# Moving conditioning passes into the opening of a decoder layer, and loading x by features there

## The chip, the cores and the metric

The kernel runs on one core of one Trainium2 chip. The metric is the time of one execution on the device, in microseconds (us); lower is better. Beside the median of three runs there is one execution under the profiler, and all durations below are from that one.

## What is computed

One decoder layer over 256 tokens of 2048 features. What matters here is its beginning:

```
mod = (silu(c) @ w_ada + b_ada).reshape(9, 2048)       # conditioning: 9 vectors
h = rms_norm(x, norm_ffn1) * (1 + mod[1]) + mod[0]
x = x + 0.5 * mod[2] * swiglu(h, w_ffn1_gu, w_ffn1_down)
h = rms_norm(x, norm_mix) * (1 + mod[4]) + mod[3]
x = x + mod[5] * token_mixing(h, ...)
h = rms_norm(x, norm_ffn2) * (1 + mod[7]) + mod[6]
x = x + 0.5 * mod[8] * swiglu(h, w_ffn2_gu, w_ffn2_down)
return rms_norm(x, norm_final)
```

swiglu(h) is (silu(h @ w_gate) * (h @ w_up)) @ w_down, with 5632 columns for each of gate and up. All is float32.

## The kernel before

**Products.** Every large product is made of three products in the fast float32 format (fp32r): high part by high part, low part of the activations by high part of the weights, and high part of the activations by low part of the weights (`products`, L353; the matmul is L359). Weights come by DMA from SyncE's queue into a ring of four 1 MB buffers (`raws`, tile `raw`); ScalarE casts 1024 columns to the high part (`wh`, L374), VectorE subtracts it to get the low part (`wl`, L376), into a ring of three pairs (`wsp`). One such pair, a piece, feeds 12 matmuls of 512 columns.

**Conditioning.** `w_ada` lies transposed in memory, one row block of 128 outputs by 2048 inputs (1 MB) for each of the 9 vectors and 16 feature blocks. VectorE multiplies such a row by silu(c) and sums it, in passes (`ada_pass`, L216, the instruction is L219): four passes of 512 columns for the vectors made behind other work. `conditioning` (L265) is a generator of 192 passes for the vectors 2, 4 and 3; `tick` (L317), called after each piece, takes as many steps of it as `pace["rate"]` says, and `pace["ahead"]` says how many passes ahead of its use a row is loaded. Where a row goes is said by the function handed in (`place_early`, L1179).

**The opening.** The first FFN can't start on all features at once, since mod[0] and mod[1] need 32 MB of `w_ada`. So it goes through four groups of feature blocks, 0 and 1, 2 to 5, 6 to 11, 12 to 15 (L1120). In each group the loop of L1182 visits 16 chunks of 512 columns of gate and up (`visit`, L1132), adds this group's part of the product to a partial sum (copied to and from SBUF, L1143 and L1170), and between visits the generator `group` (L1037) makes the next group's h: for each pair of feature blocks it loads four rows (`place`, L979) and sums them, scales x by the roots of the mean squares (ScalarE, L1028), turns it on TensorE into two PSUM banks (`turned_x`, L1024, four transposes, L1032), and applies scale and shift on ScalarE (`modulated`, L625). In the third group the 192-pass generator ticks as well: 48 ticks at 2/3, 32 passes, each row into `ring[1]`, one single buffer, loaded when its first pass is due. The remaining 160 passes stand behind the 117 ticks that follow: three more chunks (`ffn_up`, L1230) and most of the down product (L1234).

**Order.** SyncE's queue (weights, rows, DMA transposes) keeps the order of the program; a load whose buffer is not free holds up all that is behind it. The order on VectorE, ScalarE, TensorE and GpSimd is set by a scheduler at build time, which moves an instruction ahead where its inputs are there; some stretches (L1075, and the end of a down product) are in an order written by hand. GpSimd only issues a few DMAs here.

Of the kernel before, what the change touches and what calls it, by code (L numbers as in the profile page):

```python
# [9 lines left out]
F32 = mybir.dt.float32  # L10
# [3 lines left out]
ALU = mybir.AluOpType  # L14
# [3 lines left out]
P = 128  # L18
S = 256
D = 2048  # L20
DFF = 5632
NT = S // P
KD = D // P
# [54 lines left out]
def layer_kernel(  # L78
# [17 lines left out]
    w_ffn2_down,  # L96
    norm_final,
    consts,
    out,
):  # L100
    nc = tc.nc
    ctx.enter_context(tc.manual_schedule(engines={mybir.EngineType.SP}))
    b_ada = b_ada[0]
    one = ctx.enter_context(tc.tile_pool(name="one", bufs=1))
# [15 lines left out]
    def nm(s):  # L120
        uid[0] += 1
        return f"{s}_{uid[0]}"
# [4 lines left out]
    def bank():  # L127
        return psm.tile([P, CH], F32, tag="ps", name=nm("ps"))
# [4 lines left out]
    def t512():  # L133
        return tmp.tile([P, CH], F32, tag="t512", name=nm("t"))
# [7 lines left out]
    def small(n, tag):  # L142
        return two.tile([P, n], F32, tag=tag, name=nm(tag))
# [3 lines left out]
    ident = small_c[:, C_ID : C_ID + P]  # L147
# [43 lines left out]
    def columns_rest():  # L191

        pt = bank()
        n, at = 2 * KD, 9 * KD - P
        with tc.issue_after(newest[-1]):
            nc.tensor.transpose(pt[:, :n], rows[:n, 3 * P :], ident[:n, :n])
            nc.tensor.transpose(
                pt[:, P : P + at], rows[:at, 2 * P : 3 * P], ident[:at, :at]
            )
        nc.vector.tensor_copy(gains[:, 1:, :].rearrange("p g k -> p (g k)"), pt[:, :n])  # L200
        nc.vector.tensor_copy(all_b[:, P:], pt[:, P : P + at])
        for m in (4, 7):
            nc.vector.tensor_scalar_add(bcols[:, m, :], bcols[:, m, :], 1.0)
# [42 lines left out]
    def raw_row():  # L246
        raw = raws.tile([P, KB, CH], F32, tag="raw", name=nm("raw"))
        return raw.rearrange("p k n -> p (k n)")
# [59 lines left out]
    pace = {"steps": iter(()), "rate": 0.0, "due": 0.0, "behind": None}  # L308

    def set_pace(outputs, halves, place, ahead):  # L310
        assert next(pace["steps"], None) is None
        pace["steps"] = conditioning(outputs, place, pace["behind"])
        pace["rate"] = len(outputs) * KD * AQ / halves
        pace["due"] = 0.0
        pace["ahead"] = ahead
# [64 lines left out]
    cast, low, newest = [], [], []  # L380
# [188 lines left out]
    def flat_tile():  # L569

        return flat.tile([P, CH], F32, tag="flat", name=nm("flat"))
# [53 lines left out]
    def modulated(h, k, src, m_shift):  # L625

        nc.scalar.activation(
            h, src, AF.Identity,
            bias=modc[:, m_shift, k : k + 1], scale=modc[:, m_shift + 1, k : k + 1],
        )  # L630
# [332 lines left out]
    ring = [tiles[0][:, :D], tiles[0][:, D:]]  # L963
# [13 lines left out]
    rows_of, alone = {}, [False]  # L977

    def place(m, k):  # L979
        if k < 1:  # L980
            rows_of[m, k] = raw_row()
        else:
            if not alone[0]:
                ring.reverse()
            rows_of[m, k] = ring[0]
        ada_load(m, k, rows_of[m, k], 2 if k < 2 else 1)
# [23 lines left out]
    r = small(NT, "rs2")  # L1010
# [13 lines left out]
    def turned_x(k0):  # L1024

        xn = [t512()[:, : 2 * P] for _ in range(NT)]
        for t in range(NT):
            nc.scalar.mul(xn[t], x_sb[:, t, k0 * P : (k0 + 2) * P], r[:, t : t + 1])  # L1028
        turned = [bank()[:, :S] for _ in range(2)]
        for i in range(2):  # L1030
            for t in range(NT):
                nc.tensor.transpose(  # L1032
                    turned[i][:, t * P : (t + 1) * P], xn[t][:, i * P : (i + 1) * P], ident
                )
        return turned

    def group(ks, passes=2):  # L1037

        for k0 in ks[::2]:
            for k in (k0, k0 + 1):  # L1040
                for m in (1, 0):
                    if (m, k) not in rows_of:
                        place(m, k)
                    for q in range(passes):
                        ada_pass(k, rows_of[m, k], early[m], q, passes)
                    yield
            for m in (1, 0):
                ada_end(m, slice(k0, k0 + 2), early[m], 0 if m else None, passes)
            h = t512()
            for i, src in enumerate(turned_x(k0)):  # L1050
                modulated(h[:, i * S : (i + 1) * S], k0 + i, src, 0)
            parts_of_h(held, k0, h)

# [21 lines left out]
    with tc.manual_schedule(engines=ORDERED):  # L1075
# [10 lines left out]
        for ci in (2, 3):  # L1086
# [5 lines left out]
            out=v, in_=ssq.rearrange("p (t c) -> p t c", t=NT), axis=AX.X, op=ALU.add  # L1092
        )
        nc.vector.tensor_scalar(
            out=v, in0=v, scalar1=1.0 / D, scalar2=EPS, op0=ALU.mult, op1=ALU.add
# [6 lines left out]
            out=r, in0=q, scalar=-3.0, in1=r, op0=ALU.add, op1=ALU.mult  # L1102
# [18 lines left out]
    groups = [range(a, b) for a, b in zip(bounds, bounds[1:])]  # L1121
# [10 lines left out]
    def visit(n, ks, ends, ticks=False, ends_all=False):  # L1132
        starts = n not in banks
        seeded = starts and n in moved and not ends_all
        if starts:
            banks[n] = [acc_bank() for _ in range(NT)]
        if starts:
            unlinted.discard(n)
        if seeded:
            unlinted.add(n)  # L1140
            for b, p in zip(banks[n], part_of(n)):
                with tc.issue_after(cast[-1]):
                    nc.scalar.copy(b, p)  # L1143
        raw_of = [(load_blocks(n, part), part) for part in (ks[:KB], ks[KB:]) if part]
        pieces = [
            (raw[:, a : a + 2, :], part[a : a + 2])
            for raw, part in raw_of
            for a in range(0, len(part), 2)
        ]
        for raw, part in pieces:  # L1150
            a, b = part[0] - ks[0], part[-1] + 1 - ks[0]
            hl = slice(part[0], part[-1] + 1)
            wh, wl = split(wsp, "w", raw[:, : len(part), :], CH)
            products(
                banks[n],
                held.hi[:, hl, :],
                held.lo[:, hl, :],
                wh,
                wl,
                starts and a == 0 and not seeded,  # L1160
                b == len(ks) and ends,
                seeded=n in unlinted,
            )
            if ticks:
                tick()
# [7 lines left out]
    ROWS_FFN1 = [(2, None, 0.5), (4, 1, None), (3, None, None)]  # L1173
    row_ring = []
# [2 lines left out]
        return row_ring[0]() if row_ring else raw_row()  # L1177

    def place_early():  # L1179
        return row_ring[0]() if row_ring else ring[1]  # L1180

    for g, ks in enumerate(groups):  # L1182
        alone.append(g == len(groups) - 2)
        del alone[:-1]
        final = g == len(groups) - 1
        if g == len(groups) - 2:
            set_pace(ROWS_FFN1, 48 * 192 // 32, place_early, 0)
        order = chunks if (len(groups) - g) % 2 else chunks[::-1]
        coming = iter(()) if final else group(groups[g + 1], 1 if g == 0 else 2)
        due = 0 if final else 2 * len(groups[g + 1])  # L1190
        stay = () if final else order[-2:]
        for i, n in enumerate(order):
            if g == 0 and n in firsts:
                continue
            visit(n, ks, n not in stay, g == len(groups) - 2, final or (g == len(groups) - 2 and n in stay))
            if final:
                turn_step()
            last = len(order) - 2
            if g == 0:
                by = [min(due, -(-j * due // 12)) for j in (i - 2, i - 1)]  # L1200
                by = by[1] - by[0]
            else:
                by = (i + 1) * due // last - i * due // last if i < last else i == last
            for _ in range(by + (g == 0 and i == last)):
                next(coming, None)
            if g == 0:
                for m in {2: firsts[:1], 3: (order[2], firsts[1])}.get(i, order[i - 1 : i]):
                    if m not in stay:
                        to_parts(m)
                if i == 3:  # L1210
                    columns_rest()
            if n in stay or g == 0:
                continue
            if not final:
                to_parts(n)
            elif n % 2:
                swiglu_up(
                    banks.pop(n - 1),
                    banks.pop(n),
                    tiles,  # L1220
                    n // 2,
                    (part_of(n - 1), part_of(n)),
                    True,
                )
    gate = gate_row()
    tiles.append(slot())
    row_ring.append(two_rows())
    pace["rate"] = (192 - 32) / 117
    pace["ahead"] = AQ
    ffn_up(held, gu, tiles, EARLY, turned=range(EARLY, DFF // CH))  # L1230
    gate_in = gate_load(gate, 2)
# [317 lines left out]
    for p in range(2):  # L1549
# [9 lines left out]
        for i in range(2):  # L1559
            for t in range(NT):  # L1560
                m = sg[:, 0, i, t, :]
                nc.vector.tensor_add(m, m, sg[:, 1, i, t, :])
                k0 = (2 * p + i) * KB
# [140 lines left out]
```

## Time and profile before

| | us |
|---|---|
| median of 3 runs (2361.89 to 2362.61) | 2361.95 |
| the profiled execution | 2361.77 |
| its span, first to last instruction | 2360.0 |
| TensorE busy | 2336.1 |
| VectorE busy | 1670.4 |
| ScalarE busy | 1377.8 |
| mean granted TensorE clock | 0.999 of full speed |

The sums below are made against the profiled execution's 2361.77 us. A busy row of TensorE says that matmuls are in its pipeline; whether they follow each other at their own rate is read from the distance between their starts. "x" is a count of instructions; in brackets behind a timeline row stands the time that the engine was idle before it, and who released it.

### The profile page before, as it was taken

Reading aid. Unit: us, or ns where it says so; the run is one execution under the profiler, and the core shown is the slowest. Engines: PE = TensorE matmul, PEld = TensorE weight load, DVE = VectorE, ACT = ScalarE, POOL = GpSimd, SP = SyncE. Lnnn points to the kernel's source line nnn. Section 1 sums busy time; section 2 is a strip of 40 time slices with the busy share of each in tenths; the row PEclk is TensorE's granted clock in tenths of the full one; section 3 lists DMA queues with packets and bytes.
Section 4 is the critical chain, followed back from the end, with each engine's and each line's share of the span. In section 5 each row is a group of like instructions: output and inputs, shape, how many; then the busy total and the mean of one; then the engine's idle time right before and its main releaser. Section 6 shows DMA issues by size and latency. Waiting matters only on the chain.

```text
span 2360.0 us, 28359 instructions
## 1 busy us (share of the span) xinstructions
PE 2336.1 (99%) x10447; PEld 1917.4 (81%) x10447; DVE 1670.4 (71%) x2576; ACT 1377.8 (58%) x1907; POOL 9.2 (0%) x21
## 2 busy tenths in 40 slices
PE   8999999999999999999999999999999999999998
PEld 5888888888888888778888888888888888888887
DVE  7877778878977768976777876676555555555656
ACT  6776577555556568774556564465455455455544
POOL 0000000000000000000000000000000000000000
PEclk9999999999999999999999999999999999999999
DMA  9988759999776888866778787754767777776553
GB/s 378 374 319 323 301 174 335 384 367 342 299 270 232 281 276 240 264 213 245 278 281 293 295 290 294 282 205 179 253 234 258 244 241 263 225 231 203 194 196 125
DMA packets 194765, 629.98 MB, mean 267 GB/s; under 512 B 117249, under 2 KB 117633, under 8 KB 124097
## 3 DMA queue, kind: packets, MB, share of 16 engines
q1 hardware_dynamic: 192130, 617.14, 74.5%
q0 software_dynamic: 1600, 9.83, 1.1%
q8 instruction: 82, 1.34, 0.2%
q10 hardware_dynamic: 896, 1.19, 0.1%
q14 instruction: 57, 0.47, 0.1%
HBM read 597.16 MB, written 4.22 MB: 255 GB/s over the span
## 4 chain that ended last, share of the span: by engine, by line
PE 95%; DMA 1%; DVE 1%; ACT 1%; issue 0%; SPq 0%; DVEq 0%; ACTq 0%
PE pa L359 93%; DMA raw<-in_w_ffn_gu_dram 1%; DVE slot L219 1%; PE ps L1389 0%; DVE wl L376 0%; DMA slot<-in_w_ada_dram 0%; ACT wh L374 0%; PE pd L1305 0%; DMA x_sb<-in_x_dram 0%; PE ps L359 0%; ACT slot L550 0%; PE ps L893 0%; ACT slot L1170 0%; PE ps L1305 0%; PE pd L1489 0%
## 5 line engine op out<-in xcount | busy, mean ns | idle before, releaser
L376 DVE TENSOR_TENSOR wl<-raw,wh 128x1024 fp32r<-128x1024 f32 x792 | 960.9, 1222 | 532.2 <-ACT wh L374 466.9
L374 ACT CAST wh<-raw 128x1024 fp32r<-128x1024 f32 x792 | 829.6, 1054 | 811.1 <-PE pa L359 758.5
L359 PE MATMUL pa<-wh,hh 128*128 128x512 f32 x2184 | 593.5, 392 | 3.5 <-ACT wh L374 2.7
L359 PE MATMUL pa<-wh,hl 128*128 128x512 f32 x2184 | 588.1, 389 | 0.0
L359 PE MATMUL pa<-wl,hh 128*128 128x512 f32 x2184 | 585.8, 390 | 0.1
L359 PEld LDWEIGHTS pa<-wh,hh 128*128 128x128 f32 x2184 | 407.2, 188 | 92.6 <-ACT wh L374 6.4
L359 PEld LDWEIGHTS pa<-wh,hl 128*128 128x128 f32 x2184 | 409.9, 188 | 86.2 <-issue 0.4
L359 PEld LDWEIGHTS pa<-wl,hh 128*128 128x128 f32 x2184 | 409.3, 188 | 86.7 <-DVE wl L376 0.8
L359 PE MATMUL pa<-wh,a 128*128 128x512 f32 x1824 | 452.4, 389 | 1.7 <-DVE a L410 1.1
L359 PEld LDWEIGHTS pa<-wh,a 128*128 128x128 f32 x1824 | 341.4, 188 | 73.2 <-DVE a L410 1.6
L359 PE MATMUL pa<-wl,a 128*128 128x512 f32 x912 | 245.1, 389 | 0.4 <-DVE wl L376 0.4
L219 DVE CUSTOM_DVE_ANT_0 slot<-slot,cact 128x512 f32<-128x512 f32 (+2 forms) x308 | 232.3, 803 | 14.6 <-DMA slot<-in_w_ada_dram 14.3
L359 PEld LDWEIGHTS pa<-wl,a 128*128 128x128 f32 x912 | 171.0, 188 | 36.2 <-DVE wl L376 0.8
L550 ACT COPY slot<-back 128x512 uint16<-128x512 uint16 x156 | 104.0, 766 | 0.0
L219 DVE CUSTOM_DVE_ANT_0 rows_x<-rows_x,cact 128x512 f32<-128x512 f32 x124 | 78.7, 686 | 13.5 <-DMA rows_x<-in_w_ada_dram 13.3
L409 ACT CAST a<-slot 128x512 fp32r<-128x512 f32 x114 | 70.6, 620 | 29.8 <-PE pa L359 29.8
L534 ACT COPY flat<-t 128x512 uint16<-128x512 uint16 x144 | 81.3, 617 | 8.0 <-DVE t L1462 5.6
L410 DVE TENSOR_TENSOR a<-slot,a 128x512 fp32r<-128x512 f32 x114 | 77.8, 684 | 0.2 <-ACT a L409 0.2
L219 DVE CUSTOM_DVE_ANT_0 raw<-raw,cact 128x512 f32<-128x512 f32 (+1 forms) x72 | 47.9, 716 | 12.1 <-DMA raw<-in_w_ada_dram 12.0
L1170 ACT COPY slot<-pa 128x512 f32<-128x512 f32 x72 | 38.6, 590 | 17.8 <-PE pa L359 17.6
L359 PE MATMUL pa<-wh,home 128*128 128x512 f32 x160 | 39.5, 389 | 0.0
L219 DVE DVE_READ_ACCUMULATOR2_ANT sums<- 128x1 f32 x440 | 35.9, 82 | 0.0
(223 smaller groups left out, 1077.6 us busy)
## 6 DMA issues: line engine op xcount, KB each, us to landing
raw<-in_w_ffn_gu_dram SPq DMA_DIRECT2D x160, 1024.0 KB, 5.2
raw<-in_w_in_dram SPq DMA_DIRECT2D x104, 1024.0 KB, 5.7
slot<-in_w_ada_dram SPq DMA_DIRECT2D x92, 1024.0 KB, 7.3
raw<-in_w_ffn_down_dram SPq DMA_DIRECT2D x88, 1024.0 KB, 4.9
rows_x<-in_w_ada_dram SPq DMA_DIRECT2D x31, 1024.0 KB, 7.0
raw<-in_w_ada_dram SPq DMA_DIRECT2D x17, 1024.0 KB, 5.5
raw<-in_w_swa_branch_dram SPq DMA_DIRECT2D x16, 1024.0 KB, 4.9
raw<-in_w_ret_branch_dram SPq DMA_DIRECT2D x16, 1024.0 KB, 4.9
```

The source lines that it names most:

```text
L219: nc.vector.tensor_tensor_reduce(out=w[:, at], in0=w[:, at], in1=cact[:, at], scale=1.0, scalar=0.0, op0=ALU.mult, op1=ALU.add, accum_out= ...
L359: product = nc.tensor.matmul(banks[t], act[:, j, t * P : (t + 1) * P], weights[:, j, :], start=starts and i == 0 and j == 0, stop=ends and ...
L374: cast.append(nc.scalar.copy(hi, src).ins)
L376: low.append(nc.vector.tensor_sub(lo, src, hi.bitcast(F32)).ins)
L409: nc.scalar.copy(hi, v)
L410: nc.vector.tensor_sub(lo, v, hi.bitcast(F32))
L534: nc.scalar.copy(planes[:, i, :], words(src)[:, :, i])
L550: nc.scalar.copy(into[:, :, :, i], held["turned"][:, i])
L1170: nc.scalar.copy(p, b)
```

## The change

The 192 passes for vectors 2, 4 and 3 are dealt out anew: 48 in the third group (one a tick, still through `ring[1]`), 16 in the first 12 visits of the last group (two in three ticks, each row into the next of the four weight buffers, loaded one pass ahead), 128 behind. From feature block 6 on (five pairs), x is no longer scaled on ScalarE and turned on TensorE: a transposed copy of x is given to the kernel as one more input, a pair of blocks is loaded from it by one 256 KB DMA of SyncE (`normed_columns`), and GpSimd multiplies it by a row of the roots. That row is made once, in the first group (`roots_in_rows`): two scalings of the identity on ScalarE, a fill on GpSimd, one plain float32 matmul of 256 columns, one copy.

```diff
--- before.py
+++ after.py
@@ -96,6 +96,7 @@
     w_ffn2_down,
     norm_final,
     consts,
+    x_t,
     out,
 ):
     nc = tc.nc
@@ -1034,9 +1035,36 @@
                 )
         return turned
 
+    TURNED = 6
+    root_row = []
+
+    def roots_in_rows():
+
+        root_row.append(one.tile([P, D], F32, tag="row", name="root_row")[:, :S])
+        diag = t512()
+        for t in range(NT):
+            nc.scalar.mul(diag[:, t * P : (t + 1) * P], ident, r[:, t : t + 1])
+        full = flat_tile()[:, :P]
+        nc.gpsimd.memset(full, 1.0)
+        rows_ps = bank()
+        with tc.issue_after(newest[-1]):
+            nc.tensor.matmul(rows_ps[:, :S], full, diag[:, :S], start=True, stop=True)
+        nc.scalar.copy(root_row[0], rows_ps[:, :S])
+
+    def normed_columns(k0):
+
+        xt = t512()
+        both = xt.rearrange("p (k s) -> p k s", s=S)
+        nc.sync.dma_start(both, x_t[k0 : k0 + 2].rearrange("k p s -> p k s"))
+        nc.gpsimd.tensor_tensor(
+            out=both, in0=both, in1=root_row[0][:, None, :].broadcast_to([P, 2, S]), op=ALU.mult
+        )
+        return [xt[:, i * S : (i + 1) * S] for i in range(2)]
+
     def group(ks, passes=2):
 
         for k0 in ks[::2]:
+            srcs = normed_columns(k0) if k0 >= TURNED else None
             for k in (k0, k0 + 1):
                 for m in (1, 0):
                     if (m, k) not in rows_of:
@@ -1047,7 +1075,7 @@
             for m in (1, 0):
                 ada_end(m, slice(k0, k0 + 2), early[m], 0 if m else None, passes)
             h = t512()
-            for i, src in enumerate(turned_x(k0)):
+            for i, src in enumerate(srcs or turned_x(k0)):
                 modulated(h[:, i * S : (i + 1) * S], k0 + i, src, 0)
             parts_of_h(held, k0, h)
 
@@ -1177,14 +1205,18 @@
         return row_ring[0]() if row_ring else raw_row()
 
     def place_early():
-        return row_ring[0]() if row_ring else ring[1]
+        if row_ring:
+            return row_ring[0]()
+        return ring[1] if alone[0] else raw_row()
 
     for g, ks in enumerate(groups):
         alone.append(g == len(groups) - 2)
         del alone[:-1]
         final = g == len(groups) - 1
         if g == len(groups) - 2:
-            set_pace(ROWS_FFN1, 48 * 192 // 32, place_early, 0)
+            set_pace(ROWS_FFN1, 192, place_early, 0)
+        if final:
+            pace["rate"], pace["ahead"] = 2 / 3, 1
         order = chunks if (len(groups) - g) % 2 else chunks[::-1]
         coming = iter(()) if final else group(groups[g + 1], 1 if g == 0 else 2)
         due = 0 if final else 2 * len(groups[g + 1])
@@ -1192,7 +1224,7 @@
         for i, n in enumerate(order):
             if g == 0 and n in firsts:
                 continue
-            visit(n, ks, n not in stay, g == len(groups) - 2, final or (g == len(groups) - 2 and n in stay))
+            visit(n, ks, n not in stay, g == len(groups) - 2 or final and i < 12, final or (g == len(groups) - 2 and n in stay))
             if final:
                 turn_step()
             last = len(order) - 2
@@ -1209,6 +1241,8 @@
                         to_parts(m)
                 if i == 3:
                     columns_rest()
+                if i == 5:
+                    roots_in_rows()
             if n in stay or g == 0:
                 continue
             if not final:
@@ -1225,7 +1259,7 @@
     gate = gate_row()
     tiles.append(slot())
     row_ring.append(two_rows())
-    pace["rate"] = (192 - 32) / 117
+    pace["rate"] = (192 - 64) / 117
     pace["ahead"] = AQ
     ffn_up(held, gu, tiles, EARLY, turned=range(EARLY, DFF // CH))
     gate_in = gate_load(gate, 2)
@@ -1679,6 +1713,7 @@
     arrays, args = {}, []
     given = {n: inputs[n] for n in _INS}
     given["consts"] = constants()
+    given["x_t"] = _np.asarray(given["x"])[0].T.reshape(KD, P, S)
     given["w_ada"] = _np.asarray(given["w_ada"])[0].T
     for name in _BY_CHUNK:
         w = _np.asarray(given[name])
```

## Rows read from the trace of the kernel before

**Rows 1.** The page, part 1: busy time and share of the span by engine.

```profile
PE 2336.1 (99%) x10447; PEld 1917.4 (81%) x10447; DVE 1670.4 (71%) x2576; ACT 1377.8 (58%) x1907; POOL 9.2 (0%) x21
```

**Rows 2.** The page, part 4: the chain of work that ended last.

```profile
PE 95%; DMA 1%; DVE 1%; ACT 1%; issue 0%; SPq 0%; DVEq 0%; ACTq 0%
```

**Rows 3.** Busy time by stretch: third group, last group, passes behind; columns in the first line.

```profile
core 0: us, PE busy (x) PEld busy (x) DVE busy (x) ACT busy (x) POOL busy (x), PEclk, DMA share, GB/s
157.00:285.00 128.00, 128.00 (x568) 105.84 (x567) 94.58 (x151) 78.33 (x108) 0.00 (x0) 1.00 0.84 318
285.00:372.00 87.00, 87.00 (x386) 72.03 (x385) 63.03 (x74) 59.62 (x79) 0.00 (x0) 1.00 0.66 201
372.00:690.00 318.00, 314.74 (x1382) 258.25 (x1381) 268.65 (x498) 179.51 (x225) 2.10 (x4) 1.00 0.94 344
```

**Rows 4.** TensorE's waits, 372 to 690 us: total us, times, longest.

```profile
PE pa L359 <- DVE a L410: 1.1, 1, 1.1
PE pa L359 <- ACT wh L374: 1.0, 1, 1.0
PE pa L359 <- DVE t L642: 0.6, 1, 0.6
PE pa L359 <- DVE wl L376: 0.4, 1, 0.4
```

**Rows 5.** VectorE's timeline ahead of 523 us: start, us, what.

```profile
520.37 0.69 DVE L219 CUSTOM_DVE_ANT_0 slot<-slot,cact 128x512 f32<-128x512 f32 x1
...
522.82 1.29 DVE L410 TENSOR_TENSOR a<-slot,a 128x512 fp32r<-128x512 f32 x2
```

**Rows 6.** Instructions of line 219, 372 to 690 us, busy on VectorE.

```profile
372.00:690.00 318.00, 101.68 (x320) 1.00 0.94 344
```

**Rows 7.** TensorE's timeline around two sets of turned x.

```profile
64.76 0.60 PE L1032 MATMUL ps<-small_c,t 128*128 128x128 f32 x4
65.38 1.20 PE L359 MATMUL pa<-wh,hh 128*128 128x512 f32 x4
...
102.68 1.08 PE L359 MATMUL pa<-wl,hh 128*128 128x512 f32 x4
103.59 0.60 PE L1032 MATMUL ps<-small_c,t 128*128 128x128 f32 x4
103.95 0.70 PE L359 MATMUL pa<-wh,hh 128*128 128x512 f32 x2
104.50 0.63 PE L359 MATMUL pa<-wh,hl 128*128 128x512 f32 x2
```

**Rows 8.** Tile x_sb: the scaling on ScalarE (ns min/median/max).

```profile
L1028 ACT ACTIVATE t<-x_sb,rs x16: 493/518/524, 14.0 to 212.9; 128x256 f32<-128x256 f32 x16
```

**Rows 9.** TensorE's timeline in the opening: plain float32 products, and a wait.

```profile
20.87 1.88 PE L1070 MATMUL pd<-raw,t 128*128 128x512 f32 x4
...
53.34 1.20 PE L359 MATMUL pa<-wh,hh 128*128 128x512 f32 x4 [0.97 <-ACT wh L374]
```

**Rows 10.** SyncE's queue in the third group: row and weight loads.

```profile
161.44 0.42 SPq L214 DMA_DIRECT2D slot<-in_w_ada_dram  x1
...
244.62 0.92 SPq L214 DMA_DIRECT2D slot<-in_w_ada_dram  x2
248.65 3.05 SPq L1129 DMA_DIRECT2D raw<-in_w_ffn_gu_dram  x2
258.29 0.33 SPq L214 DMA_DIRECT2D slot<-in_w_ada_dram  x1
```

**Rows 11.** VectorE's timeline in the third group: first pass of two rows, and a burst's end.

```profile
172.06 0.68 DVE L219 CUSTOM_DVE_ANT_0 slot<-slot,cact 128x512 f32<-128x512 f32 x1
...
252.30 0.69 DVE L219 CUSTOM_DVE_ANT_0 slot<-slot,cact 128x512 f32<-128x512 f32 x1 [0.96 <-DMA slot<-in_w_ada_dram]
...
254.75 1.22 DVE L376 TENSOR_TENSOR wl<-raw,wh 128x1024 fp32r<-128x1024 f32 x1
```

**Rows 12.** ScalarE's waits, 157 to 285 us (this is all of them).

```profile
ACT wh L374 <- PE pa L359: 52.8, 34, 3.5
```

## Prediction

> **What bounds the kernel now.** I read the page's busy times first: TensorE is busy for 99% of the span, VectorE for 71%, ScalarE for 58%, GpSimd for nothing that counts [rows 1]. The chain of waits agrees: 95% of it is TensorE, 1% each DMA and VectorE [rows 2]. So time falls only where TensorE is given less to do or waits less. What it has to do is fixed by the matmuls: in the timeline four of them start 0.91 us after the four before, 0.227 us each [rows 7], and a piece of twelve takes 2.72 us.
>
> Where it waits is seen in the busy times by stretch [rows 3]. In the third group (157 to 285 us) and the last (285 to 372 us) it is busy throughout. In the 318 us in which the other 160 passes lie, it is busy for 314.74, so 3.26 us are idle, and the list of its waits shows four of them, three on VectorE (1.1, 0.6 and 0.4 us) and one on ScalarE's cast (1.0) [rows 4]. VectorE's own timeline tells what stood in front: four conditioning passes in a row from 520.37 to 522.82 us, 2.45 us, and only then the low part that the matmul at 523 us wants [rows 5]. VectorE is busy for 268.65/318 = 84% in that stretch, for 94.58/128 = 74% in the third group and 63.03/87 = 72% in the last [rows 3]. That is the pattern to hold on to: at 74% no stall, at 84% one per cent of the time.
>
> **The change, part by part.**
>
> *Turned x.* Five pairs of feature blocks lose four transposes each. One set starts at 103.59 us, the next matmul at 103.95, and that one's pair takes 0.55 us where 0.455 is usual: 0.36 + 0.10 = 0.46 us of TensorE's time. The one at 64.76 us takes 0.62 before the next matmul starts, with the same 0.1 behind it 0.72 [rows 7]. The other three look like the one at 103.59 or are spread out for a little less. I take 0.72 + 4 x 0.45 = 2.5 us off TensorE, all on the path. ScalarE loses ten scalings of 0.52 us, 5.2 us [rows 8], which it doesn't need: its only waits in the third group are on TensorE [rows 12]. That list is also what hides the DMA that replaces them: no weight load is late there, and an x load of 256 KB is a quarter of a row load. It is issued ahead of the pair's four rows, and its buffer is one of five that turn; the instruction that used it last belongs to an earlier pair, so SyncE isn't held by it.
>
> *The root row.* One plain float32 matmul of 256 columns: 512 columns take 1.88/4 = 0.47 us [rows 9], so 0.24, and 0.1 as after a transpose; at most 0.34 us. ScalarE gets three small instructions, at most 0.52 us each [rows 8]. The lower end is nothing, as TensorE waits in the first group anyway (0.97 us at 53.34, behind a cast whose data came late) [rows 9]. I take 0.3 us for all of it; the ends are 0 and 1.9.
>
> *GpSimd's multiply.* No row shows one. The nearest is a pass of VectorE over the same 512 columns, also with two inputs, 0.69 us [rows 11]; the other bound is the 2.45 us of a burst, which is the length of VectorE work that has stopped TensorE [rows 5]. As x comes ahead of four rows of conditioning, even 2.45 us on GpSimd is waited for by nobody; I take nothing, if the two engines don't disturb each other (a rival).
>
> *32 passes leave the stretch behind the opening.* 160 passes cost 101.68 us there, 0.635 each [rows 6], so 20.3 us go and VectorE falls to 248.3/318 = 78%. Between no waits at 74% and 3.26 us at 84.5%, a straight line leaves 0.4 of them, 1.3 us: 1.9 us won, and 0.1 us of slow restart, as behind a transpose [rows 7], at each of three waits, 2.2 us in all. The ends: nothing, since it is the burst of four and not the mean that stops TensorE, and 3.7 us.
>
> *They come into the opening.* The third group gets 16 more, 10.2 us, and goes to 104.8/128 = 82%; the last gets 16, and goes to 73.2/87 = 84%. By the same line that is 1.0 us of new waits in the third group and 0.8 in the last. The lower end is nothing, since these groups have been free of waits so far; the upper end is the rival on the row buffer. In the last group each row takes one of the four weight buffers for its landing and its burst, and weight loads behind it in SyncE's queue wait for that; as DMA is at 0.66 and a visit takes 5.4 us, three buffers still reach 16 us ahead, and I add nothing.
>
> *Rows and DMA.* 4 MB more and two x loads in 128 us raise the third group from 318 GB/s to about 353, at a share of 0.84 now [rows 3]. In the stretch behind it is 0.94 at 344 GB/s, where one cast of 1.0 us is all that TensorE waits for on that account [rows 3, 4], so this is near the limit but not over it.
>
> Sum: 2361.77 - 2.5 + 0.3 - 2.2 + 1.8 = 2359.2 us; I say **2359.0**. The median of the runs is 0.18 us above the profiled execution, which changes nothing.
>
> **The rivals.**
>
> *All waits go and none come (2355.4 us).* VectorE's order is set anew by the scheduler over the whole stretch, and the bursts are fewer by a fifth. Then 2.5 + 3.7 us come off and the 0.2 of the opening hide: 2361.77 - 6.2 = 2355.6, or 2354 if the wait in the first group at 53 us goes with them. For it: three of the four waits stand right behind bursts [rows 4, 5], and 84% is not far above what gives none. Against: the opening takes up what the rest gives.
>
> *The single row buffer becomes the bound (slower, about 2369 us).* The third group needs 12 rows in 16 visits, one in 10.9 us, through `ring[1]`, and a row is loaded only when the burst on the one before is over. From issue at 244.62 to the first pass at 252.30 is 7.7 us, and the burst ends 2.45 us later: a cycle of 10.2 [rows 10, 11]. From issue at 161.44 to 172.06 it is 10.6, a cycle of 13.1. While a row waits at the head of SyncE's queue, the weight loads behind it wait too. At 13.1 the rows fall 12 x 2.2 = 26 us behind. The queue already stands before the row issued at 258.29, some 6.6 us after the weight loads ahead of it were out (248.65 + 3.05), and TensorE doesn't stop [rows 3, 10], so 6.6 us are covered. It decides from a cycle of 10.9 + 6.6/12 = 11.4 us on; at 12.2 us it costs 15.6 - 6.6 = 9 to 10 us, 2369. Against it: at 161 us VectorE wasn't hurried, and at 252 us it stood waiting for the row 0.96 us, which is the shorter cycle.
>
> *Nothing but the transposes (2361.3 us).* Bursts stay four passes long wherever they lie, so the stretch behind keeps its 3.26 us, and the opening gets its 1.8: 2361.77 - 2.5 + 0.3 + 1.8.
>
> *GpSimd stops VectorE (2364 us).* Beside VectorE's 74 to 82% in the opening, each of five multiplies would hold up a subtraction by 0.69 to 2.45 us, and like the bursts stop TensorE for 0.4 to 1.1 [rows 4, 5]; five at 1 us make 2359 + 5. Against: only three of 40 bursts behind the opening stopped it on VectorE's account. The Trainium skill, SBUF — State Buffer, section Who interferes with whom, states that a VectorE instruction with two SBUF inputs and a GpSimd instruction that reads SBUF exclude each other for the whole instruction. The trace before has no GpSimd arithmetic, so no row bears on it. From the Trainium skill, GPSIMD Engine Reference, section 3.1 (4497 ns for 2048 columns) one multiply would be estimated at 1.1 to 1.2 us, and five at some 6 us of VectorE's time.
>
> **How the numbers follow.** A measurement of this kernel can tell about 0.2%, 4.7 us, from no change, so faster is below 2357.2 and slower above 2366.7. Forecast (2357 to 2361) 0.38; all waits go 0.25; only the transposes 0.18; the row buffer 0.14; GpSimd 0.05. Faster is the second case and the lower edge of the first, 0.30; slower is most of the row buffer's, 0.14; the rest, 0.56, is the same. The range reaches from 2354, where the second case ends, to 2366, which holds the forecast, the transposes alone and GpSimd, and leaves out the row buffer and the edge below.
>
> **What would show it.** In the profile after, the transposes of line 1032 are fewer by 20, and TensorE has no wait in their place; GpSimd shows five multiplies, whose length settles that term; VectorE's busy time is up by some 10 us in each of the last two groups and down by 20 behind; the waits behind bursts between 372 and 690 us are fewer than four. If TensorE waits on casts in the third group and ScalarE waits there on weight DMAs, the row buffer has decided. If a subtraction that takes 1.22 us now is longer while GpSimd works, that rival has. The forecast is wrong if the waits between 372 and 690 us are as before, or if more than 2 us are idle in the opening.

## The result, and the profile after

The changed kernel takes 2365.88 us (median of 22 runs, 2362.80 to 2367.88) against 2362.17 us before (22 runs, 2361.37 to 2363.51): a ratio of 1.0014, 95% interval 1.0008 to 1.0020. It is slower, by 3.7 us, where 2.8 us faster was forecast; the difference is clear of the noise, and less than the 4.7 us that the prediction counted as a change. The runs after spread over 5.1 us, those before over 2.1; a likely cause of that is given further down. Now and then one execution is far longer (in the experiments below, four in all, of 2605 to 6066 us): the ratios leave these out, the medians don't. The profiled execution after took 2364.32 us, 1.6 us under its median, with a span of 2362.4 us, 2.4 more than before.

Busy times by stretch, in the stretches of [rows 3] and one more ahead of them, the second group (columns: the stretch, its length, then busy time of TensorE, its weight loads, VectorE, ScalarE and GpSimd, the granted clock, DMA's share, GB/s):

```profile
68.00:157.00 89.00, 85.24 (x375) 69.98 (x374) 71.51 (x99) 64.40 (x97) 5.54 (x3) 1.00 0.92 357
157.00:285.00 128.00, 126.41 (x556) 103.76 (x555) 105.80 (x186) 75.68 (x104) 3.11 (x2) 1.00 0.88 344
285.00:372.00 87.00, 86.93 (x384) 71.60 (x383) 70.08 (x105) 56.22 (x74) 0.00 (x0) 1.00 0.83 250
372.00:690.00 318.00, 315.68 (x1388) 259.84 (x1388) 252.28 (x436) 181.60 (x228) 2.16 (x4) 1.00 0.89 321
```

VectorE's load has moved as the change says: up by 11 us in the third group and 7 in the last, down by 16 behind. But TensorE is now idle for 3.76 us in the second group, where no pass was added and where the same stretch of the kernel before has none:

```profile
68.00:157.00 89.00, 89.00 (x400) 73.66 (x399) 72.54 (x107) 67.46 (x104) 0.00 (x0) 1.00 0.92 355
```

TensorE's waits of the whole execution after, of which 1.7 us stand in the first group as before, 3.8 in the second (two of 1.9), 1.4 in the third, and 2.3 behind the opening (all these in the first row; the rows of lines 1033, 177 and 1098 lie within the first 28 us, and the last one, as before, behind 690 us):

```profile
PE pa L360 <- ACT wh L375: 9.1, 7, 2.3
PE ps L1033 <- ACT t L1029: 4.3, 1, 4.3
PE pa L177 <- DMA c_row<-in_c_dram: 2.6, 1, 2.6
PE pa L1098 <- ACT t L628: 2.3, 2, 1.8
PE pa L360 <- DVE slot L1591: 0.6, 1, 0.6
```

The three waits on VectorE of [rows 4] are gone. Every new one is on ScalarE's cast of a weight. The two in the second group look alike. This is TensorE around the first, and then ScalarE:

```profile
101.78 1.07 PE L360 MATMUL pa<-wl,hh 128*128 128x512 f32 x4
104.72 1.20 PE L360 MATMUL pa<-wh,hh 128*128 128x512 f32 x4 [1.88 <-ACT wh L375]
105.76 0.62 PE L360 MATMUL pa<-wh,hl 128*128 128x512 f32 x2
```

```profile
97.22 1.07 ACT L1198 COPY slot<-pa 128x512 f32<-128x512 f32 x2 [0.44 <-PE pa L360]
98.17 0.63 ACT L636 CAST hh<-t 128x512 fp32r<-128x512 f32 x1
98.69 1.12 ACT L1171 COPY pa<-slot 128x512 f32<-128x512 f32 x2
102.66 1.07 ACT L1198 COPY slot<-pa 128x512 f32<-128x512 f32 x2 [2.84 <-PE pa L360]
103.61 2.01 ACT L375 CAST wh<-raw 128x1024 fp32r<-128x1024 f32 x2
```

From 99.8 to 102.66 us ScalarE does nothing. What it waits for is TensorE's end of the current chunk, since the copy-out of that chunk's partial sum (L1198) is next in its order; the cast that TensorE will want right after stands behind it. So TensorE ends the chunk, and then waits for two copies and a cast: 1.88 us of idle time. From start to start the four matmuls at 101.78 us take 2.94 us where 0.91 is usual, and the next four 1.04, so 2.16 us are lost. The kernel before has at this place both casts among the copies back into PSUM (L1143), and the copy-out (L1170) behind them:

```profile
99.75 0.63 ACT L1143 COPY pa<-slot 128x512 f32<-128x512 f32 x1
100.27 1.08 ACT L374 CAST wh<-raw 128x1024 fp32r<-128x1024 f32 x1
101.22 0.63 ACT L1143 COPY pa<-slot 128x512 f32<-128x512 f32 x1
101.74 1.08 ACT L374 CAST wh<-raw 128x1024 fp32r<-128x1024 f32 x1
103.56 1.08 ACT L1170 COPY slot<-pa 128x512 f32<-128x512 f32 x2 [0.74 <-PE pa L359]
```

In the changed kernel the copy-out has moved ahead of the casts. This swap is there twice, at 102.66 and 132.03 us, once behind each of the first two pairs of feature blocks that come by features; no line of the change asks for it.

### The profile page after: what moved, and what is told of

Its sections match the earlier page's. It is cut to its first block, busy times and chain, and to the rows that moved or that the text cites. A ratio compares the mean times of both kernels' runs of the same rounds, so it can differ in the third digit from the quotient of the medians.

```text
span 2362.4 us, 28340 instructions
## 1 busy us (share of the span) xinstructions
PE 2335.1 (99%) x10429; PEld 1916.7 (81%) x10429; DVE 1673.5 (71%) x2576; ACT 1373.2 (58%) x1900; POOL 18.1 (1%) x27
## 4 chain that ended last, share of the span: by engine, by line
PE 82%; DMA 1%; DVE 1%; ACT 0%; issue 0%; DVEq 0%; ACTq 0%; SPq 0%
PE pa L360 80%; DMA raw<-in_w_ffn_gu_dram 1%; PE ps L1423 0%; PE pd L1339 0%; PE ps L360 0%; PE ps L894 0%; ACT wh L375 0%; DVE wl L377 0%; PE ps L1339 0%; PE pd L1523 0%; PE pd L1508 0%; PE pd L1522 0%; PE pd L1521 0%; DVE t L709 0%; DVE rows_x L220 0%
## 5 line engine op out<-in xcount | busy, mean ns | idle before, releaser
L220 DVE CUSTOM_DVE_ANT_0 slot<-slot,cact 128x512 f32<-128x512 f32 (+2 forms) x292 | 224.1, 818 | 11.2 <-DMA slot<-in_w_ada_dram 10.9
L220 DVE CUSTOM_DVE_ANT_0 raw<-raw,cact 128x512 f32<-128x512 f32 (+1 forms) x88 | 58.2, 712 | 14.2 <-DMA raw<-in_w_ada_dram 14.0
L1198 ACT COPY slot<-pa 128x512 f32<-128x512 f32 x72 | 38.7, 589 | 31.2 <-PE pa L360 31.1
```

Source lines behind the costliest of these rows:

```text
L220: nc.vector.tensor_tensor_reduce(out=w[:, at], in0=w[:, at], in1=cact[:, at], scale=1.0, scalar=0.0, op0=ALU.mult, op1=ALU.add, accum_out= ...
L1198: nc.scalar.copy(p, b)
```

## The experiments

Theory A: the cost is that order on ScalarE, brought about by x by features. Theory B: it is the passes moved into the opening. Theory C: GpSimd's multiply holds VectorE up, passes end later, rows and weights are loaded later, and whatever order ScalarE had it would wait. Each kernel below was timed in five rounds beside the kernel before on the same chip: the first four experiments on one chip, where the kernel before took 2362.17 us, the other four on another, where it took 2361.95.

### x by features alone

```diff
-            set_pace(ROWS_FFN1, 192, place_early, 0)
-        if final:
-            pace["rate"], pace["ahead"] = 2 / 3, 1
+            set_pace(ROWS_FFN1, 48 * 192 // 32, place_early, 0)
...
-            visit(n, ks, n not in stay, g == len(groups) - 2 or final and i < 12, ...)
+            visit(n, ks, n not in stay, g == len(groups) - 2, ...)
...
-    pace["rate"] = (192 - 64) / 117
+    pace["rate"] = (192 - 32) / 117
```

> The change's second half alone: x by features from block 6 on, multiplied on GpSimd; the 192 passes dealt out as before (32 in the third group, none in the last, 160 behind). Theory A (ScalarE's order): both waits of 1.88 us near 104 and 134 us are here, since in ScalarE's order of this kernel the copy-out of a chunk stands ahead of the next chunk's casts at the same two places; TensorE then loses about 4.0 us there against 2.5 us won on transposes: time about 2362.2 - 2.5 + 4.0 = 2363.7, and some 3 us of waits behind the opening as before. Theory B (the passes in the third and last group are what costs): no wait between 68 and 157 us, time about 2359.7.

Measured: 2364.20 us against 2362.17, ratio 1.0008 (0.9999 to 1.0017). TensorE's waits between 68 and 157 us are, to the digit, those of the changed kernel:

```profile
PE pa L360 <- ACT wh L375: 3.8, 2, 1.9
```

Behind the opening the three waits on VectorE (1.1, 0.6, 0.4 us) are back. This half of the change brings the new waits; theory B can't explain them, and its 2359.7 lies below the interval. The time itself isn't clear of that of the kernel before.

### The passes alone

```diff
-            srcs = normed_columns(k0) if k0 >= TURNED else None
+            srcs = None
...
-                if i == 5:
-                    roots_in_rows()
```

> The change's first half alone: passes 48, 16 and 128, x scaled on ScalarE and turned on TensorE as before. Theory A: no wait between 68 and 157 us; the waits of the third group (about 1.5 us) and of the stretch behind (about 2.3 us, in place of 3.3) as in the changed kernel; the 2.5 us of transposes stay: time about 2362.2 + 1.5 - 1.0 = 2362.7. Theory B: 2364 or more.

Measured: 2362.51 us against 2362.17, ratio 1.0001 (0.9993 to 1.0010). No wait between 68 and 157 us, one of 1.9 us in the third group, one of 2.0 behind the opening in place of four. The one in the third group is the same picture: ScalarE stands for 6.87 us until a chunk is done, copies it out, and only then casts.

```profile
274.65 1.07 ACT L1198 COPY slot<-pa 128x512 f32<-128x512 f32 x2 [6.87 <-PE pa L360]
275.61 2.01 ACT L375 CAST wh<-raw 128x1024 fp32r<-128x1024 f32 x2
```

### The changed kernel, with the copy-out one visit later

The partial sum of a chunk is now copied out after the next chunk's visit in the program (from the second group on). Two chunks' sums fill the four PSUM banks of this kind, and the visit after that needs two of them.

```diff
+            while late and g:
+                to_parts(late.pop(0))
             if n in stay or g == 0:
                 continue
             if not final:
-                to_parts(n)
+                late.append(n)
```

> The changed kernel, but a chunk's partial sum is copied out one visit later in the program, so that ScalarE's order has the next chunk's casts ahead of it. Theory A: the two waits near 104 and 134 us go, and the one near 251 us, where a copy-out also stands ahead of casts, goes or shrinks; 4 to 5.5 us less than the changed kernel, about 2361. Theory C (GpSimd's multiply holds VectorE and so the row and weight loads up, and the weights are late whatever ScalarE's order): the waits stay at about half or more of 1.88 us, 2364 to 2366.

Measured: 2357.37 us against 2362.17, ratio 0.9980 (0.9971 to 0.9989): 8.5 us less than the changed kernel, more than theory A's 4 to 5.5, and faster than the kernel before. Of the 8.5, 6.75 us lie between the two profiled executions (4.3 in the second group, about 1 each in the third and behind the opening); the rest is that the changed kernel's median is 1.6 us above its profiled execution. ScalarE at the same place:

```profile
98.43 0.63 ACT L636 CAST hh<-t 128x512 fp32r<-128x512 f32 x1
98.95 1.12 ACT L1171 COPY pa<-slot 128x512 f32<-128x512 f32 x2
99.99 2.01 ACT L375 CAST wh<-raw 128x1024 fp32r<-128x1024 f32 x2
102.91 1.08 ACT L1198 COPY slot<-pa 128x512 f32<-128x512 f32 x2 [0.91 <-PE pa L360]
```

The cast starts at 99.99 us with no wait for its data: the weights were there. In the changed kernel the same cast started at 103.61 because of its place in the order, not for want of data: by that trace the load that it needs was issued at 89.04 us and had landed at 96.61. TensorE is busy throughout the second group; 0.4 us of waits are left in the third, where ScalarE's cast at 246.91 us waits 5.26 us for a weight load, and 1.1 behind the opening:

```profile
68.00:157.00 89.00, 89.00 (x394) 73.68 (x393) 76.27 (x108) 66.22 (x99) 5.18 (x3) 1.00 0.92 364
157.00:285.00 128.00, 127.44 (x560) 104.53 (x559) 105.61 (x180) 76.39 (x105) 3.02 (x2) 1.00 0.90 353
372.00:690.00 318.00, 316.74 (x1393) 260.90 (x1393) 249.87 (x432) 180.32 (x224) 2.16 (x4) 1.00 0.88 318
```

### The changed kernel, with the multiplies on VectorE

```diff
-        nc.gpsimd.tensor_tensor(
+        nc.vector.tensor_tensor(
             out=both, in0=both, in1=root_row[0][:, None, :].broadcast_to([P, 2, S]), op=ALU.mult
```

> The changed kernel with the five multiplies on VectorE (0.69 us each) in place of GpSimd. Theory A: the order on ScalarE decides; if it is the same, both 1.88 us waits stay and the time is that of the changed kernel, 2365.9 within 1 us. Theory C: without GpSimd's hold on VectorE the passes end sooner (the pass that took 2.32 us takes 1.22), weights come about 1 us sooner, and the waits near 104 us shrink by 1 us or more: 2363 to 2364.5.

Measured: 2366.05 us against 2362.17, ratio 1.0016 (1.0007 to 1.0026), the changed kernel's time. The two waits in the second group are there unchanged, 3.8 us in two. Theory C is out as a cause of the waits. GpSimd does hold VectorE up, though. In the changed kernel's trace this is a multiply on GpSimd, and under it two conditioning passes on VectorE:

```profile
91.82 2.27 POOL L1059 TENSOR_TENSOR t<-t,root_row 128x512 f32<-128x512 f32 x1 [20.52 <-PE pa L360]
```

```profile
91.71 1.22 DVE L220 CUSTOM_DVE_ANT_0 slot<-slot,cact 128x1024 f32<-128x1024 f32 x1
92.85 2.32 DVE L220 CUSTOM_DVE_ANT_0 slot<-slot,cact 128x1024 f32<-128x1024 f32 x1
```

The multiply starts under the first pass, which ends at 92.93 us, and ends at 94.09; the second pass takes 2.32 us instead of 1.22 and ends at 95.17, 1.08 us after the multiply. So the multiply and the second pass did their work one after the other. By the Trainium skill, SBUF — State Buffer, section Who interferes with whom, the two exclude each other for a whole instruction; this row agrees. The multiplies take 1.30 to 2.27 us, 1.73 in the mean. This hold costs TensorE nothing that these runs show.

### The late copy-out on the kernel before

The edit of the third experiment on the kernel before.

> The kernel before with the late copy-out alone. If the late copy only mends what the change had broken, it gains nothing here, since the kernel before has no wait between 64 and 372 us: 2362.2 within 0.7. If it is worth something by itself (for instance because ScalarE's order behind the opening comes out better), 2360 or less.

Measured: 2361.57 us against 2361.95, ratio 0.9998 (0.9989 to 1.0007). By itself the late copy is worth nothing: the kernel before had no copy-out in front of a cast that mattered.

### x by features with the late copy-out, passes as before

Both edits, of the first and the third experiment, on the changed kernel.

> x by features from block 6 on with the late copy-out, passes as before. Theory A: the two waits at 101 and 131 us are gone, what is left is the transposes' 2.5 us and what TensorE's clock lost behind a wait: 2362.2 - 2.5 = 2359.7, 4.5 us below the version without the late copy (2364.2). If the x loads or GpSimd cost something of their own, 2361 or more.

Measured: 2358.08 us against 2361.95, ratio 0.9982 (0.9973 to 0.9991), and 6.1 us under the same kernel without the late copy. Against the late copy alone it is 3.5 us: TensorE's waits behind the opening are 2.3 us here and 3.4 there, so 1.1 us is that, and 2.4 us is left for the transposes and the root row. Theory A's 2359.7 was 1.6 us too high, mainly for this 1.1.

### The passes with the late copy-out, x turned as before

Both edits, of the second and the third experiment, on the changed kernel.

> Passes 48, 16 and 128 with the late copy-out, x turned on TensorE as before. Theory A: the wait of 2.0 us at 274 us, where a copy-out stands ahead of casts in the version without the late copy, shrinks to what the late weights leave, under 1 us; 1.5 to 2.5 us below that version's 2362.5, so 2360 to 2361. If the single row buffer decides, the wait stays at about 2 us and so does the time.

Measured: 2360.94 us against 2361.95, ratio 0.9996 (0.9987 to 1.0005), 1.6 us under the passes alone. TensorE waits for nothing in the third group, with 48 passes through the single buffer:

```profile
157.00:285.00 128.00, 128.00 (x567) 105.54 (x566) 104.14 (x181) 78.11 (x108) 0.00 (x0) 1.00 0.89 345
```

So at 104 of 128 us VectorE costs TensorE nothing, and neither does the row buffer.

### The kernel before, with the order swapped in four places

```diff
-        cast.append(nc.scalar.copy(hi, src).ins)
+        if behind_copy:
+            with tc.issue_after(behind_copy.pop()):
+                cast.append(nc.scalar.copy(hi, src).ins)
+        else:
+            cast.append(nc.scalar.copy(hi, src).ins)
...
                 to_parts(n)
+                if g == 1 and i in (3, 6, 9, 12):
+                    behind_copy.append(last_out[0])
```

(`last_out` holds the copy-out's last instruction.)

> The kernel before, with ScalarE's order changed in four visits of the second group alone: the first cast of the next chunk is held until the chunk's copy-out is done. Theory A: each place makes TensorE wait 1.9 us and 0.1 to restart, 8 us in all, and where the granted clock falls to half behind a wait, 1.6 us more; 2370 to 2376. If such an order is harmless by itself and only late weights make the wait, within 2 us of 2362.2.

Measured: 2371.76 us against 2361.95, ratio 1.0040 (1.0027 to 1.0052): 9.8 us. The order is harmful by itself. TensorE's waits in the second group, of which the kernel before has none there:

```profile
PE pa L359 <- ACT wh L376: 6.6, 4, 1.9
```

The first and the third of them (the last three numbers of a stretch are the granted clock, DMA's share and GB/s):

```profile
91.39 1.07 PE L359 MATMUL pa<-wl,hh 128*128 128x512 f32 x4
94.34 1.92 PE L359 MATMUL pa<-wh,hh 128*128 128x512 f32 x4 [1.88 <-ACT wh L376]
96.05 1.91 PE L359 MATMUL pa<-wh,hl 128*128 128x512 f32 x4
97.75 1.19 PE L359 MATMUL pa<-wl,hh 128*128 128x512 f32 x4
```

```profile
132.07 1.07 PE L359 MATMUL pa<-wl,hh 128*128 128x512 f32 x4
132.98 0.60 PE L1036 MATMUL ps<-small_c,t 128*128 128x128 f32 x4
135.02 1.20 PE L359 MATMUL pa<-wh,hh 128*128 128x512 f32 x4 [1.44 <-ACT wh L376]
```

```profile
89.00:91.00 2.00, 2.00 (x11) 1.65 (x10) 1.67 (x6) 0.00 (x0) 0.00 (x0) 1.00 1.00 397
94.00:96.00 2.00, 1.66 (x4) 1.34 (x5) 1.68 (x2) 2.00 (x4) 0.00 (x0) 0.64 0.94 369
96.00:98.00 2.00, 2.00 (x6) 1.58 (x5) 2.00 (x4) 2.00 (x4) 0.00 (x0) 0.51 1.02 426
98.00:100.00 2.00, 2.00 (x10) 1.63 (x10) 2.00 (x3) 2.00 (x5) 0.00 (x0) 1.00 0.94 270
```

At each of the four places the matmuls start 2.04 us late, 8.2 us in all. At the last two of them (135.02 and 153.51 us) a set of transposes that the kernel needs anyway runs in that time, so the idle time is 1.44 us and not 1.88; two sets at 0.36 us [rows 7] make 0.7 of the 8.2. Behind the first two waits the clock falls: the granted clock is 0.51, the 1.2 GHz level, and by 98 us it is back at 2.4. Four matmuls take 1.71 us from start to start instead of 0.91, twice: 1.6 us lost, and as much again behind the wait at 114.90 us. Behind the two waits of 1.44 us the granted clock stays at 1.00. Together that is 8.2 - 0.7 + 3.2 = 10.7 us; 0.7 us less is idle behind the opening, and the span is 10.0 us longer.

## Why the prediction was wrong

The time lies inside the stated range of 2354 to 2366, by 0.1 us. That is luck: the upper end was put there to hold the rivals up to GpSimd's (2364), and GpSimd cost nothing. The prediction's own sign of being wrong came: more than 2 us idle in the opening, where 5.4 us were (3.76, 1.59 and 0.07 in the last three groups).

**Turned x** (2.5 us off): right, 2.4 us. In the changed kernel line 1033 has 12 transposes where line 1032 had 32, and no wait in their place. What failed is the sentence on ScalarE, that it loses 5.2 us of scalings "which it doesn't need". I took its order as given and counted only its work. Taking instructions out of it, and an input that comes by another way, changed which of a copy-out and a cast the scheduler put first. A rival of the prediction says that VectorE's order is set anew, and counts on it for a gain; nowhere does it ask what the same does on ScalarE. It also looked at ScalarE's waits in the third group alone [rows 12], while the new waits came in the second. This is the step that was wrong: a change of ScalarE's order was put at nothing. The waits in the second group cost 2 x 2.16 = 4.3 us, more than the transposes gave.

**The root row** (0.3 us): about right. The plain product holds TensorE for 0.42 us, from its start to that of the next instruction, where at most 0.34 was put, and TensorE is idle about as long between 28 and 68 us as before (1.79 us, 1.83 before). No run takes the root row out alone.

```profile
38.45 0.59 PE L1051 MATMUL ps<-t,flat 128*128 128x256 f32 x2
38.87 0.38 PE L1033 MATMUL ps<-small_c,t 128*128 128x128 f32 x2
```

**GpSimd's multiply** (nothing): right in the time, and the rival fell, though the hold on VectorE is real. The sign that the prediction named for this rival came, and decided nothing: beside the multiply at 69.33 us a subtraction took 1.73 us instead of 1.22, and TensorE didn't wait for it.

```profile
70.65 1.73 DVE L377 TENSOR_TENSOR wl<-raw,wh 128x1024 fp32r<-128x1024 f32 x1 [0.51 <-ACT wh L375]
```

**Passes out of the stretch behind** (2.2 us): too much. The three waits on VectorE went, as expected, but one of 2.28 us on a late weight came; idle time fell from 3.26 to 2.32 us, by 0.9. That cast waits for its data:

```profile
401.32 0.96 PE L360 MATMUL pa<-wh,hh 128*128 128x512 f32 x3 [2.28 <-ACT wh L375]
```

```profile
400.23 1.99 ACT L375 CAST wh<-raw 128x1024 fp32r<-128x1024 f32 x2 [5.75 <-DMA raw<-in_w_ffn_gu_dram]
```

```profile
382.60 0.43 SPq L215 DMA_DIRECT2D slot<-in_w_ada_dram  x1
388.80 1.24 SPq L540 DMA_TRANSPOSE back<-flat  x1
390.10 0.57 SPq L351 DMA_DIRECT2D raw<-in_w_ffn_gu_dram  x1
```

SyncE's queue issued nothing from 383.0 to 388.8 us, then a DMA transpose and the load at 390.10, which landed 10 us later and released the cast. What held the queue before that transpose wasn't looked into. A wait like it stood at 423 us before (1.0 us in [rows 4]). With the late copy-out 0.7 us is the longest there. Why it grows with the passes and shrinks with the late copy wasn't tried further.

**Passes into the opening** (1.8 us): 1.59 us idle in the third group and 0.07 in the last, close in size and wrong in cause. The straight line from VectorE's load doesn't hold: at 104 of 128 us there is no wait when ScalarE's order is right (the passes with the late copy-out). Of the 1.4 us near 253 us, 0.4 stays with the late copy-out where x comes by features, behind a late weight load.

**The row buffer** fell. In the trace after, bursts of four passes start at 236.78 and 244.95 us, 8.2 us apart, where I had put the cycle at 10.2 at least from [rows 10, 11]. The row for the second burst was issued at 239.35 us, so it took 5.6 us from issue to first pass, where [rows 10, 11] have 7.7: two rows picked out of the trace gave no measure of the shortest cycle.

In sum, against 2359.0: 4.3 us for the waits in the second group and 1.3 for the stretch behind make 5.6, where the profiled execution lies 5.3 above; with 1.6 for the median's distance from that execution, 6.9 was measured. For that last part the clock is the likely cause, since one fall of it costs as much, and it fits the spread: the trace after shows no fall of the clock behind its waits, but with the same waits of 1.88 us that of x by features alone shows one (behind the wait that ends at 133.79 us, not behind the one at 104.42) and that of the multiplies on VectorE two. Behind the second wait of x by features alone, and behind the first with the multiplies on VectorE (this row has TensorE alone: busy time, granted clock, DMA's share, GB/s):

```profile
136.00:138.00 2.00, 2.00 (x6) 1.52 (x6) 2.00 (x4) 1.72 (x2) 0.00 (x0) 0.50 0.78 328
```

```profile
106.00:108.00 2.00, 2.00 (x7) 0.50 1.01 426
```

The 22 runs fit: the seven at a mean granted clock of 0.999 have a mean of 2364.5 us, the twelve at 0.998 have 2365.9, the three at 0.997 have 2366.6. No run forced the clock alone, so the share of each wait isn't separated.

With the order put right, the change gains more than was forecast: 2357.37 us, 4.8 under the kernel before, of which x by features with the late copy-out gives 3.9 (2361.95 to 2358.08) and the passes the other 0.9, which these intervals don't separate from nothing. Why the scheduler swapped the copy-out and the cast is open. It isn't GpSimd, since with the multiplies on VectorE the same waits are there, and it isn't the passes, since they are there without them. (One slip of the prediction: the first rival's heading has 2355.4 us where its own sum gives 2355.6.)

## What to carry to other kernels

Where a scheduler orders an in-order engine, taking work off it is not free: look at what stands ahead of what the bottleneck wants next, above all an instruction that itself waits for the bottleneck (here the copy-out of a sum that TensorE is still making). Such an instruction belongs behind the casts of the next piece, and the program can be written so that it can't be put elsewhere: one visit later, which cost nothing on the kernel before, where the buffers allowed it. When runs of a kernel spread more than those of the one before, look for waits on the engine whose granted clock falls in some of its traces.

## What the runs showed of the hardware

A wait of 1.88 us on TensorE may be followed by eight matmuls at half the clock, some 3.4 us, which cost 1.6 us more; the same wait is followed by it at some places and not at others (with x by features alone one of two, in the changed kernel's trace none of two, with the multiplies on VectorE both). A multiply of 128x512 on GpSimd took 1.30 to 2.27 us, and a VectorE pass with two SBUF inputs beside it 1.10 us longer than alone.
